# Seven products in more k-groups of two feed-forwards, later flips, output chunks between the pairs

## The chip, the cores and the metric

One core of one Trainium2 chip runs the whole program. The metric is device time in microseconds, the median of a few runs. The engines are TensorE (PE; its weight loads are listed as PEld), VectorE (DVE), ScalarE (ACT), GpSimd (POOL) and SyncE (SP), which issues the DMAs.

## What is computed

Two transformer blocks on 256 tokens of width 2048 in float32, one after the other, on the same `x`. The first block is a sliding-window attention and a SwiGLU feed-forward. The second is a hybrid mixer (gated linear attention and a pooling branch), a cross attention over a memory of 256 rows, a feed-forward with a short convolution, and a last normalisation. The change touches the two feed-forwards, both of width 5632:

```python
def swiglu(h, w_gate, w_up, w_down):
    return (jax.nn.silu(h @ w_gate) * (h @ w_up)) @ w_down

def conv_glu_ffn(h, w_up, conv_w, conv_b, w_down):
    u = h @ w_up
    u = lax.conv_general_dilated(u, conv_w[:, None, :], ...) + conv_b
    gate, val = u[..., :D_FF_2], u[..., D_FF_2:]
    return (jax.nn.silu(gate) * val) @ w_down
```

## The kernel before

**Float32 as three products.** Every large operand is split into a high part, rounded to the fp32r type, and the rest. `mm` (line 263) issues three matmuls for one k-tile of 128 rows and one half of the tokens (128): high x high, high x rest, rest x high (lines 270 to 272), each with 512 columns of weights as the moving operand.

**Units, tasks and ticks.** The weights come in units of 1 MB (512 rows of k by 512 columns). `plan` writes down the order of all units by hand, once; `load_ahead` issues their DMAs on SP into four raw buffers. Half a unit is a task: `split_ahead` casts it (ScalarE, line 225, into `wh`) and subtracts (VectorE, line 226, into `wl`), into five buffers each, three tasks ahead of the one in use. TensorE's order is the order of the code. The order of the other engines is made by a planner from priorities and modelled durations. Small work (transposes, softmax, convolution) runs as jobs: generators that are stepped once per `tick`, one tick per k-tile of the matrix multiplication, or per product. A job that yields 3 is stepped again three ticks later.

**A feed-forward before.** Its 11 chunks of 512 hidden columns each need a gate chunk and an up chunk (4 units each, the four k-groups of the width 2048). `PARTS1` and `PARTS2` group the chunks; after each group of hidden chunks, the four output chunks of the group before are computed (`w_dn1`, `w_dn2`, one unit per hidden chunk of the group) and added to `x` (`add_x`, line 451). The last group's output chunks go with the next norm or the end of the program.

**The pair.** In the first feed-forward, chunks 1 to 10 are computed by `pair`: gate and up chunk together, into four PSUM banks `p2`, `p4`, `p5`, `p3`. With A the activations of one k-group cut into token halves and k halves, and the units of gate and up as the columns, one k-group is a two by two product of blocks. In groups 0 to 2 it is taken with eight block products, in the last group with seven (Strassen's scheme in Winograd's form): sums and differences of blocks of activations (`differences`, once per feed-forward) and of weights (`form`, lines 242 to 246, four operations of VectorE in place in the raw buffers) are multiplied in seven products of two k-tiles each, one task each. Three of the products go to further banks (two `aux`, one `po`), are added with the four accumulators in the order of lines 357 to 373, and give silu's input and the up rows in four tiles. In `swiglu`, line 787 applies silu and line 774 multiplies; `group_job` then turns the rows (four transposes of TensorE in `flip`, line 405, twice) and splits them (lines 387, 388). It first yields 3.

**The second feed-forward before** uses `gemm` with plain groups for all its chunks. ScalarE scales the rows out of PSUM (line 420); `conv_job` waits 3 ticks, turns the rows, and does the taps (lines 1139 to 1142), silu, the product (line 1154) and the split.

**Buffers that the change touches.** PSUM has four banks `acc`, three `aux`, one `po`. The pool `s4` has 21 tiles of 4 KB per partition (groups of activations, sums of activations), `s2` has 12 tiles of 2 KB (rows, results of the pair, results of the convolution).

Of the kernel before, what the change touches and what calls it, by code (L numbers as in the profile page):

```python
# [10 lines left out]
F32 = mybir.dt.float32  # L11
F32R = mybir.dt.float32r
I32 = mybir.dt.int32
AF = mybir.ActivationFunctionType
# [69 lines left out]
class _Net:  # L84
# [71 lines left out]
    def units(w, n, ks=range(4)):  # L156
        return [(w, n, k) for k in ks]

    def plan(self):
# [7 lines left out]
        def pair(a, b):  # L167
            for g in range(len(a)):
                if g == len(a) - 1:
                    self.seven.add(len(p))  # L170
                p.extend((b[g], a[g]))

        def ffn(gate, up, off, down, parts, seven=False):
            prev = None
            for ks in parts:
                for c in ks:
                    if seven and c:
                        pair(U(gate, c), U(up, c + off))
                    else:
                        add([U(gate, c), U(up, c + off)], c == 0)  # L180
                if prev:
                    add([U(down, n, prev) for n in range(4)])
                prev = ks
            add([U(down, n, prev) for n in range(4)])

        add([U("w_qkv", n) for n in (4, 0, 1, 2, 3)])
        add([U("w_o", n) for n in range(4)], True)
        ffn("w_gate", "w_up1", 0, "w_dn1", PARTS1, True)
# [9 lines left out]
        ffn("w_up2", "w_up2", 11, "w_dn2", PARTS2)  # L198
        return p

    def load_ahead(self, n):
# [86 lines left out]
                    done(banks[c])  # L288
                self.tick()

    def differences(self, acts):


        nc = self.nc
        out = []
        for g, z in enumerate(acts):
            h, l = z = self.need(z)
            f = self.s4([128, 4, 256])
            nc.vector.tensor_add(f, h.bitcast(F32), l.bitcast(F32))
            p, q = f[:, :, 0:128], f[:, :, 128:256]  # L300
            yield 2
            if g < len(acts) - 1:
                hl = self.s4([128, 2, 4, 128], F32R)
                nc.vector.tensor_sub(p, p, q)
                nc.scalar.copy(hl[:, 0], p)
                nc.vector.tensor_sub(hl[:, 1], p, hl[:, 0].bitcast(F32))
                out.append((hl[:, 0], hl[:, 1]))
            else:
                s = self.s4([128, 8, 128])
                nc.vector.tensor_add(s[:, 0:2], q[:, 0:2], q[:, 2:4])  # L310
                nc.vector.tensor_sub(s[:, 2:4], s[:, 0:2], p[:, 0:2])
                nc.vector.tensor_sub(s[:, 4:6], p[:, 0:2], q[:, 0:2])
                nc.vector.tensor_sub(s[:, 6:8], p[:, 2:4], s[:, 2:4])
                yield 1
                h, l = (self.s4([128, 8, 128], F32R) for _ in range(2))
                nc.scalar.copy(h, s)
                nc.vector.tensor_sub(l, s, h.bitcast(F32))
                out.append((h, l))
            yield 2
        return out  # L320

    def pair(self, left, right, acts, diffs):

        nc = self.nc
        acts = [self.need(z) for z in acts]
        p2, p4, p5, p3 = (self.bank(tag="acc") for _ in range(4))
        last = len(acts) - 1  # L330
        for g in range(last):
            for units in (right, left):
                for k, w in enumerate(self.weights(units[g])):
                    f = g == 0 and k == 0
                    if units is left:
                        self.mm(p2, acts[g], k, 0, w, f, False)
                        self.mm(p4, acts[g], k, 1, w, f, False)
                    else:
                        self.mm(p5, acts[g], k, 1, w, f, False)
                        self.mm(p3, diffs[g], k, 0, w, f, False)  # L340
                    self.tick()
        assert self.stream[self.used:self.used + 2] == [right[last], left[last]]
        self.used += 2
        A, S = acts[last], diffs[last]

        def product(o, z, k, t, start):
            h, l = self.task()
            for i in range(2):
                self.mm(o, z, k + i, t, (h[:, i], l[:, i]), start and i == 0, i == 1)
            self.tick()  # L350

        add = nc.vector.tensor_add
        u, a, b, c = (self.s2([128, 512]) for _ in range(4))
        product(p3, S, 6, 0, False)
        o = self.bank()
        product(o, A, 0, 0, True)
        nc.scalar.copy(u, o)
        product(p2, A, 2, 0, False)
        add(a, p2, u)
        yield a  # L360
        o = self.bank()
        product(o, S, 2, 0, True)
        add(u, o, u)
        product(p5, S, 0, 0, False)
        add(b, p5, u)
        add(b, p3, b)
        yield b
        o = self.bank(tag="po")
        product(o, S, 4, 0, True)
        add(u, o, u)  # L370
        product(p4, A, 2, 1, False)
        add(c, p4, u)
        add(u, p5, u)
        yield c
        yield u
# [384 lines left out]
    def swiglu(self):  # L760
        nc, a = self.nc, self.a
        r, xacts = self.r, self.xacts

        def up(c, late):
# [12 lines left out]

            if c == 0:
                self.gemm([(self.units(w, c), f) for w, f in (("w_gate", on_gate), ("w_up1", on_up))],
                          xacts, late=late)  # L780
                diffs.append(self.spawn(self.differences(xacts)))
                return hid[0]
            diffs[0] = self.need(diffs[0])
            U = []
            for i, z in enumerate(self.pair(self.units("w_gate", c), self.units("w_up1", c), xacts, diffs[0])):
# [7 lines left out]
        self.ffn(up, "w_dn1", PARTS1, lambda *z: self.residual(*z, "g_mix_2"))  # L793

    def ffn(self, up, w, parts, last):

        prev = None
        for p in parts:
            hid = [up(c, late=c == 0) for c in p]
            if prev:  # L800
                self.residual(w, *prev, None)
            prev = (p, hid)
        last(w, *prev)


    def mixer(self):
# [320 lines left out]
    def conv_ffn(self):  # L1127
        nc, a = self.nc, self.a
        xacts, r, vec = self.xacts, self.r, self.vec
# [14 lines left out]
            return y  # L1144

        def conv_job(c, rows):
            yield 3
            hl = self.group()
            for k in (0, 2):
                yg = conv(rows[0], c, k)  # L1150
# [5 lines left out]
                yield 1  # L1156
            return hl

        def up(c, late):
            rows, hid = [], []  # L1160

            def on_gate(p):
# [2 lines left out]
            def on_val(p):  # L1165
# [1 line left out]
                hid.append(self.spawn(conv_job(c, rows)))  # L1167

            self.gemm([(self.units("w_up2", c + 11 * j), f)
                       for j, f in enumerate((on_gate, on_val))], xacts, late=late)  # L1170
            return hid[0]

        self.ffn(up, "w_dn2", PARTS2, self.final)

    def final(self, w, ks, acts):

# [115 lines left out]
```

## Time and profile before

| | us |
|---|---|
| median of 3 runs | 2728.22 (2726.79 to 2728.71) |
| profiled execution, its own time | 2726.57 |
| its span | 2724.7 |

The span goes from the first to the last instruction. A line of a timeline has the start, the duration, the engine, the line of the kernel, the operation with its output and inputs, the count, and in brackets the idle time of the engine before it and what ended that. Recorded matmuls overlap, since each starts before the end of the one before it: the distance of two starts is the time that one takes.

The stages of the span, in us from its start: the first feed-forward from about 281 to 985, the mixer and the cross attention to 1990, the second feed-forward to 2722.

### The profile page before, as it was taken

The page shows a single profiled execution, that of the slowest core. Times are in us where ns is not written, and L with a number is a line of the kernel's source. Part 1 is how long each engine was busy: PE and PEld are TensorE (multiplying, and loading weights), DVE is VectorE, ACT ScalarE, POOL GpSimd, SP SyncE. Part 2 cuts the span into 40 slices and gives each one's busy share as a digit, 9 for nine tenths or more (in the row PEclk, how much of TensorE's full clock was granted, in tenths as well). Part 3 has the DMA queues.
Part 4 walks back from the last instruction along what each step waited for, and adds up shares of the span by engine and source line. Part 5 has one row for each costly group of instructions (what it writes and reads, how often), then busy time and mean ns, then how long its engine had stood idle before and what let it go on. Part 6 is the DMA issues. An engine that isn't in the chain of part 4 may idle for free.

```text
span 2724.7 us, 31400 instructions
## 1 busy us (share of the span) xinstructions
PE 2684.9 (99%) x12472; PEld 2218.8 (81%) x12472; DVE 1669.1 (61%) x1981; ACT 1354.5 (50%) x1775; POOL 27.1 (1%) x27
## 2 busy tenths in 40 slices
PE   8999999999999999999999999999999999999998
PEld 7778888787878888888888888888888888888887
DVE  7775677767676764745545555554565656556565
ACT  6555554444444454544444455444555554554543
POOL 0000000000000000000000000000000000000000
PEclk9999999999999999999999999999999999999999
DMA  7334545555555555445555556444555555555553
GB/s 302 109 124 155 187 166 194 204 178 199 185 193 179 200 185 184 161 164 181 190 188 197 184 206 227 171 158 168 185 186 185 186 185 187 189 191 190 185 201 124
DMA packets 74083, 499.60 MB, mean 183 GB/s; under 512 B 8496, under 2 KB 9392, under 8 KB 14928
## 3 DMA queue, kind: packets, MB, share of 16 engines
q1 hardware_dynamic: 73936, 497.59, 51.1%
q8 instruction: 98, 1.61, 0.2%
q14 instruction: 49, 0.40, 0.0%
HBM read 495.46 MB, written 2.10 MB: 183 GB/s over the span
## 4 chain that ended last, share of the span: by engine, by line
PE 91%; DVE 4%; issue 2%; DMA 1%; ACT 1%; POOL 1%; SPq 0%; DVEq 0%; POOLq 0%; ACTq 0%
PE acc L270 28%; PE acc L272 28%; PE acc L271 28%; PE aux L405 2%; PE po L718 1%; DMA raw<-in_w_qkv 1%; DVE s L774 1%; POOL sm L429 1%; DMA x<-in_x 0%; PE aux L272 0%; PE aux L271 0%; PE aux L270 0%; DVE wl L226 0%; PE aux L949 0%; PE aux L679 0%
## 5 line engine op out<-in xcount | busy, mean ns | idle before, releaser
L226 DVE TENSOR_TENSOR wl<-raw,wh 128x1024 fp32r<-128x1024 f32 (+1 forms) x952 | 1160.7, 1221 | 961.1 <-ACT wh L225 959.4
L225 ACT CAST wh<-raw 128x1024 fp32r<-128x1024 f32 (+1 forms) x952 | 997.8, 1050 | 1175.8 <-PE acc L272 1154.7
L270 PE MATMUL acc<-wh,s 128*128 128x512 f32 x3600 | 1425.5, 396 | 6.5 <-ACT wh L225 5.6
L272 PE MATMUL acc<-wh,s 128*128 128x512 f32 x3600 | 1404.6, 390 | 0.6 <-DVE s L388 0.6
L271 PE MATMUL acc<-wl,s 128*128 128x512 f32 x3600 | 1403.3, 390 | 0.3 <-DVE wl L226 0.3
L270 PEld LDWEIGHTS acc<-wh,s 128*128 128x128 f32 x3600 | 676.9, 188 | 147.2 <-ACT wh L225 5.6
L272 PEld LDWEIGHTS acc<-wh,s 128*128 128x128 f32 x3600 | 676.3, 188 | 144.8 <-DVE s L388 1.1
L271 PEld LDWEIGHTS acc<-wl,s 128*128 128x128 f32 x3600 | 677.4, 188 | 134.2 <-DVE wl L226 1.4
L405 PE MATMUL aux<-con,s 128*128 128x128 f32 x408 | 63.1, 273 | 15.6 <-DVE s L774 15.6
L405 PEld LDWEIGHTS aux<-con,s 128*128 128x128 f32 x408 | 50.2, 140 | 31.5 <-DVE s L774 19.1
L420 ACT ACTIVATE s<-acc,sm 128x512 f32<-128x512 f32 x72 | 48.9, 689 | 33.3 <-PE acc L272 33.3
L451 DVE TENSOR_TENSOR x<-acc,x 128x512 f32<-128x512 f32 x96 | 61.7, 681 | 0.0
L387 ACT CAST s<-aux 128x512 fp32r<-128x512 f32 x66 | 38.3, 584 | 40.3 <-PE aux L405 30.1
L1139 ACT ACTIVATE s<-aux,vec 128x256 f32<-128x256 f32 x88 | 48.1, 560 | 13.5 <-PE aux L405 8.3
L429 POOL TENSOR_TENSOR sm<-sm,mhalf 128x2 f32<-128x2 f32 (+3 forms) x22 | 26.0, 1182 | 2691.2 <-DVE sm L437 2354.3
L388 DVE TENSOR_TENSOR s<-aux,s 128x512 fp32r<-128x512 f32 x66 | 44.7, 685 | 10.5 <-ACT s L387 9.4
L392 ACT ACTIVATE s<-aux,vec 128x256 fp32r<-128x256 f32 x80 | 37.7, 473 | 22.3 <-PE aux L405 13.9
L1140 DVE SCALAR_TENSOR_TENSOR s<-aux,vec,s 128x255 f32<-128x255 f32 x88 | 41.1, 477 | 2.6 <-ACT s L1139 0.2
L393 DVE SCALAR_TENSOR_TENSOR s<-aux,vec,s 128x256 fp32r<-128x256 f32 x80 | 38.2, 481 | 6.7 <-ACT s L392 5.4
L1142 DVE SCALAR_TENSOR_TENSOR s<-aux,vec,s 128x254 f32<-128x254 f32 x88 | 40.1, 477 | 1.2
L692 ACT ACTIVATE s<-s,sm 128x128 f32<-128x128 f32 (+1 forms) x64 | 28.3, 444 | 13.7 <-DVE sm L687 13.7
L426 ACT ACTIVATE s<-x 128x512 f32<-128x512 f32 (+1 forms) x44 | 29.1, 663 | 9.8 <-DVE x L1187 9.3
(194 smaller groups left out, 965.4 us busy)
## 6 DMA issues: line engine op xcount, KB each, us to landing
raw<-in_w_up SPq DMA_DIRECT2D x132, 1024.0 KB, 4.7
raw<-in_w_dn SPq DMA_DIRECT2D x88, 1024.0 KB, 4.8
raw<-in_w_in SPq DMA_DIRECT2D x64, 1024.0 KB, 4.7
raw<-in_w_gate SPq DMA_DIRECT2D x44, 1024.0 KB, 4.7
raw<-in_w_ckv SPq DMA_DIRECT2D x32, 1024.0 KB, 4.7
raw<-in_w_qkv SPq DMA_DIRECT2D x19, 1024.0 KB, 6.0
raw<-in_w_o SPq DMA_DIRECT2D x16, 1024.0 KB, 4.8
raw<-in_w_br SPq DMA_DIRECT2D x16, 1024.0 KB, 4.8
```

The costliest lines, as they stand in the source:

```text
L225: nc.scalar.copy(h[:, m], raw[:, m])
L226: nc.vector.tensor_sub(l[:, m], raw[:, m], h[:, m].bitcast(F32))
L270: nc.tensor.matmul(o, ah[:, k, s], h, start=first, stop=False)
L271: nc.tensor.matmul(o, ah[:, k, s], l, start=False, stop=False)
L272: nc.tensor.matmul(o, al[:, k, s], h, start=False, stop=last)
L388: nc.vector.tensor_sub(l[:, k0:k0 + n], src, h[:, k0:k0 + n].bitcast(F32))
L405: self.nc.tensor.transpose(b[:, j, t * 128:t * 128 + 128], srcs[t][:, (k + j) * 128:(k + j) * 128 + 128], self.ident)
L420: self.nc.scalar.activation(dst[t], pss[t], AF.Identity, bias=0.0, scale=sc[:, t:t + 1])
L429: self.nc.gpsimd.tensor_tensor(out, var, self.mhalf[:, :n], op=ALU.pow)
L451: nc.vector.tensor_add(xs[t], pss[t], xs[t])
L1139: nc.scalar.activation(y[:, j], b[:, j], AF.Identity, bias=bb, scale=w2)
L1140: nc.vector.scalar_tensor_tensor(y[:, j, 1:256], b[:, j, 0:255], w1, y[:, j, 1:256], op0=ALU.mult, op1=ALU.add)
```

## The change

- `SEVEN1 = (1, 3)`: in the first feed-forward's pairs, k-groups 1 and 3 are taken with seven products, where it was group 3 alone. The three further banks then accumulate over both groups (from group 1 to the end of group 3), and are read in the last.
- `SEVEN2 = (3,)`: chunks 1 to 10 of the second feed-forward are computed by `pair` too, with group 3 in seven products; ScalarE scales the four results in place. `differences` runs there once as well. Its results for plain groups lie in two tiles of `s2` each, where it was half an `s4` tile for each part.
- Both feed-forwards use the same `PARTS`, and `ffn_steps` puts the output chunks of a group between the pairs of the next group, two after each pair, where all four came after the last pair. The second feed-forward's groups have two chunks, where they had three.
- The jobs that turn the rows first yield 8, where it was 3 (except for chunk 0).

```diff
-PARTS1 = ((0,), (1, 2), (3, 4), (5, 6), (7, 8), (9, 10))
-PARTS2 = ((0, 1, 2), (3, 4, 5), (6, 7, 8), (9, 10))
+PARTS = ((0,), (1, 2), (3, 4), (5, 6), (7, 8), (9, 10))
+SEVEN1, SEVEN2 = (1, 3), (3,)
...
+    def ffn_steps():
+        prev = None
+        for ks in PARTS:
+            for i, c in enumerate(ks):
+                yield c, None, None
+                if prev:
+                    for n in range(4 * i // len(ks), 4 * (i + 1) // len(ks)):
+                        yield None, n, prev
+            prev = ks
...
-            if g < len(acts) - 1:
-                hl = self.s4([128, 2, 4, 128], F32R)
+            if g not in seven:
+                h, l = (self.s2([128, 4, 128], F32R) for _ in range(2))
...
+        o1 = None
+        for g in range(len(acts)):
+            A, S = acts[g], diffs[g]
+            if g not in seven:
+                for units in (right, left):
+                    outs = ((p2, A, 0), (p4, A, 1)) if units is left else ((p5, A, 1), (p3, S, 0))
+                    for k, w in enumerate(self.weights(units[g])):
+                        for o, z, t in outs:
+                            self.mm(o, z, k, t, w, id(o) not in used, False)
+                            used.add(id(o))
+                        self.tick()
+                continue
+            assert self.stream[self.used:self.used + 2] == [right[g], left[g]]
+            self.used += 2
+            if o1 is None:
+                o1, o6, o7 = self.bank(), self.bank(), self.bank(tag="po")
+            end = g == seven[-1]
+            product(p3, S, 6, 0, end)
+            product(o1, A, 0, 0, end)
+            if end:
+                u, a, b, c = (self.s2([128, 512]) for _ in range(4))
+                nc.scalar.copy(u, o1)
+            product(p2, A, 2, 0, end)
...
-                hid.append(self.spawn(self.group_job(silu)))
+                hid.append(self.spawn(self.group_job(silu, wait=3 if c == 0 else 8)))
...
+        for c, n, ks in self.ffn_steps():
+            if n is None:
+                hid[c] = up(c)
+                continue
+            self.gemm([(self.units(w, n, ks), lambda pss: self.add_x(n, pss, None))], [hid[k] for k in ks])
...
         def conv_job(c, rows):
-            yield 3
+            yield 3 if c == 0 else 8
...
+        def up7(c):
+            if c == 0:
+                hid = up(c)
+                diffs.append(self.spawn(self.differences(xacts, SEVEN2)))
+                return hid
+            diffs[0] = self.need(diffs[0])
+            rows = [[], []]
+            for i, z in enumerate(self.pair(self.units("w_up2", c), self.units("w_up2", c + 11),
+                                            xacts, diffs[0], SEVEN2)):
+                nc.scalar.activation(z, z, AF.Identity, bias=0.0, scale=r[:, i // 2:i // 2 + 1])
+                rows[i % 2].append(z)
+            return self.spawn(conv_job(c, rows))
```

## Rows read from the trace of the kernel before

**Rows 1.** The page: engines' busy time and instructions; the chain's shares by engine.
```profile
PE 2684.9 (99%) x12472; PEld 2218.8 (81%) x12472; DVE 1669.1 (61%) x1981; ACT 1354.5 (50%) x1775; POOL 27.1 (1%) x27
...
PE 91%; DVE 4%; issue 2%; DMA 1%; ACT 1%; POOL 1%; SPq 0%; DVEq 0%; POOLq 0%; ACTq 0%
```

**Rows 2.** Stretches: busy time and instructions per engine, granted clock, DMA share, GB/s.
```profile
281.00:985.00 704.00, 688.44 (x3065) 565.04 (x3064) 493.07 (x497) 332.71 (x350) 0.49 (x1) 1.00 0.52 189
...
1990.00:2722.00 732.00, 725.95 (x3287) 600.79 (x3286) 436.90 (x524) 368.68 (x450) 1.10 (x2) 1.00 0.52 183
2257.00:2361.00 104.00, 104.00 (x460) 86.04 (x460) 56.99 (x59) 45.13 (x48) 0.00 (x0) 1.00 0.53 188
...
283.00:325.00 42.00, 42.00 (x186) 34.68 (x186) 31.73 (x37) 22.33 (x25) 0.00 (x0) 1.00 0.52 185
```

**Rows 3.** Waits over the whole span: us in total, times, longest.
```profile
PE aux L405 <- DVE s L774: 15.6, 10, 1.6
...
PEld acc L270 <- DVE s L366: 3.5, 10, 0.4
```

**Rows 4.** Timeline of TensorE where the first pair ends and the second begins.
```profile
365.39 0.39 PE L270 MATMUL acc<-wh,s 128*128 128x512 f32 x1
...
365.84 0.39 PE L272 MATMUL acc<-wh,s 128*128 128x512 f32 x1
366.16 0.50 PE L270 MATMUL acc<-wh,s 128*128 128x512 f32 x1
...
369.72 0.27 PE L405 MATMUL aux<-con,s 128*128 128x128 f32 x1
371.55 0.55 PE L405 MATMUL aux<-con,s 128*128 128x128 f32 x3 [1.56 <-DVE s L774]
```

**Rows 5.** Timeline of TensorE at a flip of the second feed-forward.
```profile
2255.71 0.60 PE L405 MATMUL aux<-con,s 128*128 128x128 f32 x4
2256.07 0.47 PE L270 MATMUL acc<-wh,s 128*128 128x512 f32 x1
```

**Rows 6.** Timeline of TensorE: the same place after the third and the fifth pair.
```profile
478.15 0.50 PE L270 MATMUL acc<-wh,s 128*128 128x512 f32 x1
...
611.92 0.50 PE L270 MATMUL acc<-wh,s 128*128 128x512 f32 x1
```

**Rows 7.** Timeline of VectorE from the first seven-product group on.
```profile
346.27 1.23 DVE L226 TENSOR_TENSOR wl<-raw,wh 128x1024 fp32r<-128x1024 f32 x1 [1.50 <-ACT wh L225]
347.53 1.22 DVE L242 TENSOR_TENSOR raw<-raw 128x1024 f32<-128x1024 f32 x1
348.79 1.23 DVE L243 TENSOR_TENSOR raw<-raw,raw 128x1024 f32<-128x1024 f32 x1
...
360.82 1.21 DVE L226 TENSOR_TENSOR wl<-raw,wh 128x1024 fp32r<-128x1024 f32 x1
...
370.75 0.74 DVE L774 SCALAR_TENSOR_TENSOR s<-s,sm,s 128x512 f32<-128x512 f32 x1
...
377.84 1.22 DVE L226 TENSOR_TENSOR wl<-raw,wh 128x1024 fp32r<-128x1024 f32 x1 [1.38 <-ACT wh L225]
```

**Rows 8.** Timeline of ScalarE as TensorE enters that group.
```profile
356.12 1.05 ACT L225 CAST wh<-raw 128x1024 fp32r<-128x1024 f32 x1 [1.68 <-PE acc L272]
357.48 1.05 ACT L225 CAST wh<-raw 128x1024 fp32r<-128x1024 f32 x1 [0.31 <-PE acc L272]
```

**Rows 9.** Timeline of SP's queue: the loads issued during that group.
```profile
359.81 0.33 SPq L205 DMA_DIRECT2D raw<-in_w_up  x1
362.06 0.33 SPq L205 DMA_DIRECT2D raw<-in_w_gate  x1
```

**Rows 10.** DMA issues by kind: KB each, median us to landing.
```profile
raw<-in_w_up SPq DMA_DIRECT2D x132, 1024.0 KB, 4.7
```

**Rows 11.** Groups by form: busy us, mean ns of one, idle before and its releasers.
```profile
L226 DVE TENSOR_TENSOR wl<-raw,wh 128x1024 fp32r<-128x1024 f32 x948 | 1158.0, 1223 | 958.1 <-ACT wh L225 956.5
...
L243 DVE TENSOR_TENSOR raw<-raw,raw 128x1024 f32<-128x1024 f32 x10 | 12.3, 1225 | 0.3
...
L363 DVE TENSOR_TENSOR s<-aux,s 128x512 f32<-128x512 f32 x10 | 6.8, 683 | 0.0
```

More of the change, by code (lines that the diff above doesn't have):

```diff
@@ L165, in add, with pair, ffn @@
             p.extend(chunks[c][g] for c, g in self.order(chunks, late))
-        def pair(a, b):
+        def pair(a, b, seven):
             for g in range(len(a)):
-                if g == len(a) - 1:
+                if g in seven:
                     self.seven.add(len(p))
                 p.extend((b[g], a[g]))
[L173 to L184, printed above, removed]
+        def ffn(gate, up, off, down, seven):
+            for c, n, ks in self.ffn_steps():
+                if n is not None:
+                    add([U(down, n, ks)])
+                elif c:
+                    pair(U(gate, c), U(up, c + off), seven)
+                else:
+                    add([U(gate, c), U(up, c + off)], True)
+            add([U(down, n, PARTS[-1]) for n in range(4)])
         add([U("w_qkv", n) for n in (4, 0, 1, 2, 3)])
         add([U("w_o", n) for n in range(4)], True)
-        ffn("w_gate", "w_up1", 0, "w_dn1", PARTS1, True)
+        ffn("w_gate", "w_up1", 0, "w_dn1", SEVEN1)
         add([U("w_in", n) for n in (0, 1)], True)
@@ L289, in gemm, with differences @@
                 self.tick()
-    def differences(self, acts):
+    def differences(self, acts, seven):
         nc = self.nc
@@ L301, in differences @@
             yield 2
[L302 to L303 removed]
+            if g not in seven:
+                h, l = (self.s2([128, 4, 128], F32R) for _ in range(2))
                 nc.vector.tensor_sub(p, p, q)
[L305 to L307 removed]
+                nc.scalar.copy(h, p)
+                nc.vector.tensor_sub(l, p, h.bitcast(F32))
             else:
@@ L317, in differences, with pair, product @@
                 nc.vector.tensor_sub(l, s, h.bitcast(F32))
-                out.append((h, l))
+            out.append((h, l))
             yield 2
         return out
-    def pair(self, left, right, acts, diffs):
+    def pair(self, left, right, acts, diffs, seven):
         nc = self.nc
+        add = nc.vector.tensor_add
         acts = [self.need(z) for z in acts]
         p2, p4, p5, p3 = (self.bank(tag="acc") for _ in range(4))
[L330 to L346, printed above, removed]
+        used = set()
+        def product(o, z, k, t, stop):
@@ L347, in product @@
             h, l = self.task()
             for i in range(2):
-                self.mm(o, z, k + i, t, (h[:, i], l[:, i]), start and i == 0, i == 1)
+                self.mm(o, z, k + i, t, (h[:, i], l[:, i]), id(o) not in used, stop and i == 1)
+                used.add(id(o))
             self.tick()
[L352 to L371, printed above, removed]
+        o1 = None
[7 more added lines that the diff above has]
+                            self.mm(o, z, k, t, w, id(o) not in used, False)
+                            used.add(id(o))
+                        self.tick()
[11 more added lines that the diff above has]
+            product(p2, A, 2, 0, end)
+            if end:
+                add(a, p2, u)
+                yield a
+            product(o6, S, 2, 0, end)
+            if end:
+                add(u, o6, u)
+            product(p5, S, 0, 0, end)
+            if end:
+                add(b, p5, u)
+                add(b, p3, b)
+                yield b
+            product(o7, S, 4, 0, end)
+            if end:
+                add(u, o7, u)
+            product(p4, A, 2, 1, end)
@@ L762, in swiglu, with up @@
         r, xacts = self.r, self.xacts
-        def up(c, late):
+        def up(c):
             silu, hid = [], []
@@ L784, in up @@
             U = []
-            for i, z in enumerate(self.pair(self.units("w_gate", c), self.units("w_up1", c), xacts, diffs[0])):
+            for i, z in enumerate(self.pair(self.units("w_gate", c), self.units("w_up1", c),
+                                            xacts, diffs[0], SEVEN1)):
                 if i % 2 == 0:
@@ L792, in swiglu, with ffn @@
         diffs = []
[L793 to L803, printed above, removed]
+        self.ffn(up, "w_dn1", lambda *z: self.residual(*z, "g_mix_2"))
+    def ffn(self, up, w, last):
+        hid = {}
+        for c, n, ks in self.ffn_steps():
+            if n is None:
+                hid[c] = up(c)
+                continue
+            self.gemm([(self.units(w, n, ks), lambda pss: self.add_x(n, pss, None))], [hid[k] for k in ks])
+            if n == 3:
+                for k in ks:
+                    del hid[k]
+        last(w, PARTS[-1], [hid.pop(k) for k in PARTS[-1]])
     def mixer(self):
@@ L1157, in conv_job, with up @@
             return hl
-        def up(c, late):
+        diffs = []
+        def up(c):
             rows, hid = [], []
@@ L1169, in up, with last @@
             self.gemm([(self.units("w_up2", c + 11 * j), f)
-                       for j, f in enumerate((on_gate, on_val))], xacts, late=late)
+                       for j, f in enumerate((on_gate, on_val))], xacts, late=True)
             return hid[0]
-        self.ffn(up, "w_dn2", PARTS2, self.final)
+        def up7(c):
[10 more added lines that the diff above has]
+            return self.spawn(conv_job(c, rows))
+        def last(*z):
+            diffs.clear()
+            xacts.clear()
+            self.final(*z)
+        self.ffn(up7, "w_dn2", last)
     def final(self, w, ks, acts):
```

7 lines of the change are left out of this document (4 added, 3 removed).

## Prediction

> **What bounds the kernel now.** I read the page's busy times first, then a table by stretches, the list of waits, and last the timelines around one pair of chunks. The page gives TensorE 99% busy and 91% of the chain that ended last; VectorE has 61%, ScalarE 50% [rows 1]. Since recorded matmuls overlap, 99% alone proves little. The stretches do: where there is nothing but 512-column matmuls, 460 are seen in 104.00 us, one of them cut at the edge, so one starts every 104 / 459 = 0.2266 us [rows 2]. In the second feed-forward TensorE is busy 725.95 of 732 us, while VectorE works 436.90; in the first it is 688.44 of 704 with VectorE at 493.07 [rows 2]. The clock is at its upper level (1.00) in all of them. So a removed matmul is worth its 0.2266 us as long as VectorE and ScalarE, which cast the weights, stay ahead.
>
> The 15.6 us that TensorE idles in the first feed-forward are one wait, ten times: the transposes of the hidden rows (line 405) wait for VectorE's product at line 774 [rows 3]. In the first pair: the pair's last matmul ends where the next group starts, 365.39; three ticks later the first transpose starts at 369.72, the next only at 371.55, because line 774 runs at 370.75 [rows 4, 7]. A second, smaller wait sits at each pair's end: the bank that line 366 reads. The start at 365.84 is followed by one at 366.16 instead of 366.07, and the following step is slow by another 0.1: 0.2 us in all [rows 3, 4].
>
> **The change part by part.**
>
> *Matmuls.* A plain k-group of a pair is 2 units x 4 k-tiles x 2 halves of the tokens x 3 = 48 matmuls; as seven products it is 7 x 2 x 3 = 42. The first feed-forward gets a second such group in 10 pairs, the second gets one in 10 pairs: 120 matmuls go, 60 in each. 120 x 0.2266 = 27.2 us, all on the path. The matmul count should fall from 12472 to 12352. The Trainium skill ("TensorE: Matmul & The Clock Gate", Part 1, "Wait — 56ns, not 53.3ns?") gives 215.7 ns start to start for 512 columns, by which these would be worth 25.9 us; the trace's 0.2266 does not agree and decides.
>
> *Flips eight ticks on.* A tick after a pair is 6 matmuls (1.36 us). Eight instead of three put the first transpose 8 x 1.36 = 10.9 us after the pair's end instead of 4.1. Line 774 starts its second half 5.4 us after that end (370.75 - 365.39) and lasts 0.74 [rows 7], so the rows are there 4.8 us early. An unhindered flip takes 2256.07 - 2255.71 = 0.36 us for four transposes [rows 5], 0.09 each; the stalled step takes 1.83. Gain 1.74 x 10 = 17.4 us. Between 0 and 17.4, I take all of it, since the row names line 774 and nothing else. The hidden chunk is needed a whole output chunk or more later: nothing new is late.
>
> *Second seven-product group: VectorE.* It adds four combinations of weights (lines 242 to 246, 1.225 us each) and three more casts (1.22 on VectorE, 1.05 on ScalarE). One pair with its two output chunks then asks of VectorE 30 casts x 1.223 + 8 x 1.225 + the pair's end 7 x 0.68 + 1.5 (line 774) + 1.4 (line 388) + 4 x 0.68 (adds to x) = 56.9 us, while TensorE has 276 x 0.2266 + 0.9 + 0.2 = 63.6 [rows 2, 11]. It fits on average; the question is the place. In the trace the seven-product group begins on TensorE at 365.39 - 42 x 0.2266 = 355.87. VectorE starts its first cast at 346.27, 9.6 us earlier, and ends the seventh at 360.82 + 1.21 = 362.03, where TensorE needs it at 355.87 + 6 x 1.36 = 364.03: 2.0 us in hand [rows 7]. What paces the casts are the five cast buffers: ScalarE's cast at 357.48 waits for a product to free one [rows 8]. In the new order 7-product groups stand at places 1 and 3 with one plain group (10.9 us, 4 casts) between. With the first group's start as 0: VectorE is through with its seventh cast at +6.2 (no pair's end there), with the plain group's casts, again paced by buffers, by about +10.7; the third group's first cast can start when product six frees its buffer at +9.5, so it runs at +10.6 to +11.8 and the combinations at +11.8 to +17. TensorE reaches that group at +20.4, i.e. 9.8 us after that first cast, as in the trace. So the second group meets the lead that the only one has now. Cost 0; with the lead wholly lost it would be 13.5 us of VectorE work (7 casts at about 1.2, 4 combinations at 1.25) against 9.5 of TensorE: 4.0 per pair, 40 us in all. I take 0.
>
> *Its loads.* The two raw units of the second group can load only when the first group's two are free: the trace issues such loads at 359.81 and 362.06, +3.9 and +6.2, and they land 4.7 us later, at +8.6 and +10.9 [rows 9, 10]. The combination that needs the second unit follows another at about +13, so 2 us are free, and about 4 more before a product is late. Cost 0, for a landing up to 6 us slower too; nothing here can gain, as TensorE does not wait for loads today. SP's queue issues them in the same order of units; behind a waiting load stand only later loads.
>
> *The same in the second feed-forward.* Its pairs are three plain groups and one of seven, then two output chunks: what the first feed-forward does now, without a stall inside. New there: a pair ends with seven adds (ten times 4.8 us of VectorE; the copy beside them is ScalarE's), 16 more adds to x (10.9 us), the sums and differences of the activations once. That last piece stands in the stretch 283 to 325 today: VectorE 31.73 of 42, TensorE 42.00 [rows 2], so chunk 0 hides it. VectorE goes from 436.9 to about 593 of some 718 us, 83%; covered. On the path comes the bank wait at the pair's end, nearest row 0.2 us: +2.0 (0 to 2 by where the banks fall). The same wait in the first feed-forward stays.
>
> *Second feed-forward's flips.* They come in the second output chunk, four in four ticks. Now they pass without a gap. The pool of twelve 2 KB tiles then holds six of differences, four of rows and only two for the convolution; the fourth flip needs the bank of the first. Between 0 (as now) and 1.74 each (as in the first feed-forward), I take 0: the first flip's bank is free once the convolution's first output is written, and for that there is a tile.
>
> *Sum.* -27.2 - 17.4 + 2.0 = -42.6. The profiled execution took 2726.6, so 2684.0; it lies 1.6 under the median 2728.2, so a median of 2685.
>
> **Rivals.**
>
> *The gap moves.* If the flips lack a buffer rather than the data, they stall wherever they stand: -42.6 + 17.4 = -25.2, 2702. For it: it is the same length ten times. Against: the releaser is line 774 each time [rows 3], and the second feed-forward's flips use the same banks without a gap. The Trainium skill ("Perfetto Trace Analysis", Identifying the Most-Contended Engine) says that a gap repeating on the engine that should be saturated can mean too few buffers; by that rule this case holds, but the trace names data.
>
> *The second feed-forward's flips wait* for VectorE, which has two adds to x ahead of them, or for tiles: +1.74 x 10, 2702. For it: only two tiles are left. Against: lead as above.
>
> *VectorE loses part of its lead* at the second seven-product group: 1 to 2 us per pair, +10 to +20, 2695 to 2705.
>
> *Slower: VectorE paces both seven-product groups of each first-feed-forward pair.* Place: the cast of products three to seven. Price with no lead at all: 4.0 us in the first, and 4.0 + 5 x 0.60 of pair's-end adds in the second, 11 us a pair, 110 us: 2795. It turns the sign when a pair loses more than 42.6 / 10 = 4.3 us. For it: 13.5 us of VectorE work in 9.5 of TensorE, twice within 30 us. Against: VectorE is idle again at 377.84 for lack of work, 12 us after the pair's end [rows 7], and the groups are separated by plain ones.
>
> **How the numbers follow.** Forecast 0.75; the gap moves 0.05; flips of the second feed-forward wait 0.08; part of the lead lost 0.07; slower 0.05. About 5.5 us (0.2%) is what a measurement of this kernel can tell from no change; all cases but the last are far beyond it. Faster 0.93, same 0.02, slower 0.05. Range: below, 2677 (no bank wait at any pair's end, -4, and a few small steps after stalls that go too); above, 2706, which takes in the four faster cases; only the slower one is out, and stretches between.
>
> **What would show it.** Matmuls 12352. No wait of line 405 on line 774, or its successor. A pair of the first feed-forward with its two output chunks repeating every 276 x 0.2266 + 1.1 = 63.6 us, against (611.92 - 478.15) / 2 = 66.9 now [rows 6]. First feed-forward 32 us shorter at its end, second 11 to 12. TensorE waiting for line 226 or 225 inside pairs, first or second group, would show the VectorE rivals; a gap before a flip in the second feed-forward the tile one. A total above 2706, or TensorE idle over 10 us in either feed-forward, makes the prediction wrong.

## The result, and the profile after

| | before | after | difference |
|---|---|---|---|
| median of the runs shown beside each other, us | 2727.51 | 2686.98 | -40.5 |
| profiled execution: own time, span, us | 2726.57, 2724.7 | 2686.66, 2684.5 | -39.9, -40.2 |
| first feed-forward, us | 703.35 | 671.82 | -31.5 (forecast -31.0) |
| between the two, us | 994.78 | 994.78 | 0 |
| second feed-forward, us | 746.01 | 737.79 | -8.2 (forecast -11.6) |
| matmuls | 12472 | 12352 | -120 |

The ratio is 0.9852 [0.9835, 0.9869]. The forecast was 2685, so it missed by 2 us. The first feed-forward is measured here from chunk 0's first transpose to the first transpose of its last step's output chunk; the second one from the first transpose of the cross attention's last output chunk to the end of the span. The same landmarks serve for every kernel below. What stands ahead of the first one, which no edit touches, took 280.1 to 283.0 us in the traces, and the median of the kernel before was 2725.9 to 2727.5 from one batch of runs to the next; so differences of a few us are read from the feed-forwards' own times. In two of the experiments one execution took 8.4 or 11.9 ms, far outside the other runs of its kernel, and is left out.

The page after, busy times and the chain's shares, against [rows 1]:

```profile
PE 2657.9 (99%) x12352; PEld 2195.2 (82%) x12352; DVE 1890.7 (70%) x2225; ACT 1424.2 (53%) x1849; POOL 27.1 (1%) x27
...
PE 97%; DVE 2%; ACT 1%; POOL 0%; DMA 0%; issue 0%; SPq 0%; POOLq 0%; DVEq 0%; ACTq 0%
```

TensorE's busy time fell by 27.0 us, close to the 27.2 reckoned for 120 matmuls; the other 13 us are idle time that went. VectorE took on 221.6 us of work, and its share of the chain fell all the same, from 4% to 2%, while that of TensorE rose from 91% to 97%.

Stretches after (columns as in [rows 2]): the first feed-forward, then the second.

```profile
280.50:952.30 671.80, 671.80 (x3003) 553.74 (x3001) 576.40 (x570) 363.92 (x380) 0.55 (x1) 1.00 0.53 197
1952.00:2684.00 732.00, 721.35 (x3254) 593.23 (x3252) 577.23 (x697) 408.40 (x497) 1.10 (x2) 1.00 0.51 185
```

In the first, TensorE's records now cover all 671.80 us (688.44 of 704 before): the ten gaps are gone. In the second, 10.65 of 732 us are uncovered, against 6.05 before. Of these, 8.2 lie behind the last matmul (6.05 before, where the stretch ends 2.2 us nearer to it); the other 2.4 are two waits that are new. VectorE works 86% and 79%.

Waits after, the lists of TensorE and of its weight loads, against [rows 3] (us in total, times, longest):

```profile
PE aux L421 <- DVE s L1162: 1.8, 1, 1.8
...
PE acc L280 <- ACT s L315: 0.6, 1, 0.6
...
PEld acc L280 <- DVE s L382: 7.1, 20, 0.4
```

The ten waits of the transposes on line 774 (now 790) are gone. The small wait at each pair's end, 0.35 us on the weight load, came to the second feed-forward as forecast: 20 times instead of ten. The first two rows are new, both at the start of the second feed-forward's first pair; they are most of the miss there, and the experiment that asks for the differences earlier takes them apart.

TensorE after: the same place in two successive pairs of the first feed-forward, against [rows 6].

```profile
533.80 0.50 PE L280 MATMUL acc<-wh,s 128*128 128x512 f32 x1
...
597.53 0.50 PE L280 MATMUL acc<-wh,s 128*128 128x512 f32 x1
```

A pair with its two output chunks takes 63.7 us (forecast 63.6; 66.9 before).

VectorE after, as the first pair enters its second seven-product group, against [rows 7] (that group begins on TensorE at 354.06).

```profile
345.73 1.22 DVE L252 TENSOR_TENSOR raw<-raw 128x1024 f32<-128x1024 f32 x1
346.99 1.22 DVE L253 TENSOR_TENSOR raw<-raw,raw 128x1024 f32<-128x1024 f32 x1
...
359.02 1.22 DVE L236 TENSOR_TENSOR wl<-raw,wh 128x1024 fp32r<-128x1024 f32 x1
...
368.94 0.75 DVE L790 SCALAR_TENSOR_TENSOR s<-s,sm,s 128x512 f32<-128x512 f32 x1
```

The first combination starts 8.3 us before the group; before the change it was also 8.3 (347.53 against 355.87). The lead is the old one, though a second such group stands 20 us ahead. The rows' product at line 790 still ends 6.1 us after the pair's last matmul (369.69 - 363.58; 371.49 - 365.39 before); only the transpose no longer stands there waiting.

### The profile page after: what moved, and what is told of

It reads as the page before. It is cut to its first block, busy times and chain, and to the rows that moved or that the text cites. A ratio compares the mean times of both kernels' runs of the same rounds, so it can differ in the third digit from the quotient of the medians.

```text
span 2684.5 us, 31592 instructions
## 1 busy us (share of the span) xinstructions
PE 2657.9 (99%) x12352; PEld 2195.2 (82%) x12352; DVE 1890.7 (70%) x2225; ACT 1424.2 (53%) x1849; POOL 27.1 (1%) x27
## 4 chain that ended last, share of the span: by engine, by line
PE 97%; DVE 2%; ACT 1%; POOL 0%; DMA 0%; issue 0%; SPq 0%; POOLq 0%; DVEq 0%; ACTq 0%
PE acc L280 29%; PE acc L282 29%; PE acc L281 29%; PE aux L421 2%; PE aux L282 1%; PE aux L281 1%; PE aux L280 1%; PE po L734 1%; PE po L282 1%; PE po L281 1%; PE po L280 1%; PE aux L969 0%; POOL sm L445 0%; DVE wl L236 0%; DMA raw<-in_w_qkv 0%; PE aux L695 0%
## 5 line engine op out<-in xcount | busy, mean ns | idle before, releaser
L236 DVE TENSOR_TENSOR wl<-raw,wh 128x1024 fp32r<-128x1024 f32 (+1 forms) x1012 | 1230.7, 1220 | 689.0 <-ACT wh L235 677.1
L235 ACT CAST wh<-raw 128x1024 fp32r<-128x1024 f32 (+1 forms) x1012 | 1060.2, 1051 | 1084.0 <-PE acc L282 1020.6
L280 PE MATMUL acc<-wh,s 128*128 128x512 f32 x3440 | 1364.1, 397 | 7.4 <-ACT wh L235 5.5
L282 PE MATMUL acc<-wh,s 128*128 128x512 f32 x3440 | 1342.6, 390 | 0.6 <-DVE s L404 0.6
L281 PE MATMUL acc<-wl,s 128*128 128x512 f32 x3440 | 1341.0, 390 | 0.4 <-DVE wl L236 0.4
L280 PEld LDWEIGHTS acc<-wh,s 128*128 128x128 f32 x3440 | 646.9, 188 | 145.5 <-DVE s L382 7.1
L282 PEld LDWEIGHTS acc<-wh,s 128*128 128x128 f32 x3440 | 646.2, 188 | 138.1 <-DVE s L404 1.1
L281 PEld LDWEIGHTS acc<-wl,s 128*128 128x128 f32 x3440 | 647.3, 188 | 128.2 <-DVE wl L236 1.7
L467 DVE TENSOR_TENSOR x<-acc,x 128x512 f32<-128x512 f32 x112 | 72.8, 682 | 0.0
L280 PE MATMUL aux<-wh,s 128*128 128x512 f32 x120 | 46.7, 389 | 0.0
L281 PE MATMUL aux<-wl,s 128*128 128x512 f32 x120 | 46.7, 389 | 0.0
L282 PE MATMUL aux<-wh,s 128*128 128x512 f32 x120 | 46.7, 389 | 0.0
```

Source lines behind the costliest of these rows:

```text
L235: nc.scalar.copy(h[:, m], raw[:, m])
L236: nc.vector.tensor_sub(l[:, m], raw[:, m], h[:, m].bitcast(F32))
L280: nc.tensor.matmul(o, ah[:, k, s], h, start=first, stop=False)
L281: nc.tensor.matmul(o, ah[:, k, s], l, start=False, stop=False)
L282: nc.tensor.matmul(o, al[:, k, s], h, start=False, stop=last)
L467: nc.vector.tensor_add(xs[t], pss[t], xs[t])
```

## The experiments

The ratio is to the kernel before, timed beside each; differences are between the profiled spans, to the kernel before for the first one and to the kernel after for the others.

**The transposes later, alone** (on the kernel before)

```diff
-hid.append(self.spawn(self.group_job(silu)))
+hid.append(self.spawn(self.group_job(silu, wait=3 if c == 0 else 8)))
```

> The kernel before with one edit: the job that turns the hidden rows of the first feed-forward's pairs yields 8 ticks instead of 3. Theory (TensorE waited for the data of line 774, which comes 5.4 to 6.1 us after a pair's end): all ten waits go, 17.4 us less than before, about 2710. Rival (the flip lacks a buffer, the gap moves along): 2727, with a gap of about 1.7 us at the later flip.

Measured: 2708.87, 0.9937 [0.9923, 0.9950]; the span fell by 17.6 us, the median by 17.1. No wait on line 774 is left, nothing else moved, and the waits at line 366 stayed (3.5 us, ten times). That the gap went with the same number of buffers speaks for late data; alone it would also fit a buffer that comes free late. The trace of before rules that out: the four transposes of a flip go into one bank (`flip`), and the first of them was in it at 369.72, 1.83 us before the stalled three [rows 4]. The Trainium skill's rule ("Perfetto Trace Analysis", Optimization Strategy) that a repeating gap on the engine that should be saturated can mean too few buffers does not apply to this one.

**The first feed-forward's second group taken back** (on the kernel after)

```diff
-SEVEN1, SEVEN2 = (1, 3), (3,)
+SEVEN1, SEVEN2 = (3,), (3,)
```

> The changed kernel with group 3 alone in seven products in the first feed-forward (60 matmuls come back, all else stays). Theory (VectorE hides the second group wholly): 60 x 0.2266 = 13.6 us slower than the changed kernel, about 2700.5. Rival (the second group costs VectorE's lead something): less than 10 us slower.

Measured: 2700.85, 0.9906 [0.9893, 0.9920]. The span is 14.6 longer, the median 13.9, the first feed-forward 13.8 (685.59 against 671.82). In its stage the group is worth its 60 matmuls (13.6), to 0.2 us: VectorE's added work for it cost nothing there.

**The second feed-forward plain again** (on the kernel after)

```diff
-SEVEN1, SEVEN2 = (1, 3), (3,)
+SEVEN1, SEVEN2 = (1, 3), ()
...
-        self.ffn(up7, "w_dn2", last)
+        self.ffn(up, "w_dn2", last)
```

(and its chunks, but for the first, with both units of a k-group in their plain order again.)

> The changed kernel with the second feed-forward's chunks all plain again (no seven products there, its differences not computed; order of chunks and late flips stay). Theory (each matmul is worth its 0.2266 us, ten bank waits of 0.2 us and about 3.3 us at the start of that feed-forward came with the pairs): 13.6 - 2.0 - 3.3 = 8.3 us slower than the changed kernel, about 2695. Rival (VectorE's added work in the second feed-forward also costs time that no gap shows, or the start would be late anyway): 2 us slower or less, or 13 and more.

Measured: 2699.14, 0.9900 [0.9886, 0.9913]; the second feed-forward is 11.2 us longer, more than the 8.3 expected. A part is this variant's own: the first transpose of each chunk starts later than it does elsewhere,

```profile
PEld aux L421 <- issue: 5.1, 10, 0.5
```

0.27 us on TensorE, ten times: 2.7 us. Without it 8.5 remain, near the 8.2 between the kernels before and after. What makes that first transpose late is not settled.

**Output chunks after the pairs again** (on the kernel after)

```diff
-            for i, c in enumerate(ks):
+            for c in ks:
                 yield c, None, None
-                if prev:
-                    for n in range(4 * i // len(ks), 4 * (i + 1) // len(ks)):
-                        yield None, n, prev
+            if prev:
+                for n in range(4):
+                    yield None, n, prev
```

> The changed kernel with the four output chunks after the last pair of a group, as before, instead of two after each pair; the same work. Theory (VectorE is behind by some 6 us when a pair ends, one plain group of 10.9 us is all that the next pair's first seven-product group then has ahead of it, and its products four to seven come 0.5 to 2 us late): gaps of TensorE waiting for lines 236 or 235 in the second pair of five groups of the first feed-forward, none in the second one, 5 to 12 us slower than the changed kernel, 2692 to 2699. Rival (the place of the output chunks does nothing): 2687.

Measured: 2689.26, 0.9863 [0.9850, 0.9877], the span 1.6 us longer, the first feed-forward 0.6 (672.40) and the second 0.3: a miss in size. Two pairs then follow each other directly, and TensorE's weight loads do wait for casts in the second one,

```profile
PEld acc L281 <- DVE wl L236: 3.0, 9, 0.7
```

but five of these nine, 1.1 us in all and 0.2 at most, are in the first feed-forward and none in the second; the other four stand elsewhere, as four do in the kernel after (1.7 us). A loss of 5 to 12 had been expected. The order of the chunks is nearly free here.

**The transposes soon again** (on the kernel after)

```diff
-hid.append(self.spawn(self.group_job(silu, wait=3 if c == 0 else 8)))
+hid.append(self.spawn(self.group_job(silu, wait=3)))
...
-            yield 3 if c == 0 else 8
+            yield 3
```

> The changed kernel with the flips back at 3 ticks after a pair, in both feed-forwards. Theory (the wait is for the data of the pair's end, line 790 in this kernel, wherever seven products end a pair): the first feed-forward's ten gaps of 1.7 us come back, 17.4 us; in the second the rows are ready only after VectorE's seven adds and ScalarE's scaling, about 4 to 6 us after the pair's end against 4.1 us of ticks, so up to 2 us each there, 0 to 20: 17 to 37 us slower than the changed kernel, 2704 to 2724. Rival (with output chunks behind the pairs VectorE is free sooner, the flips could stand at 3): 2687.

Measured: 2724.62, 0.9993 [0.9984, 1.0002]: nearly the whole gain of the change is gone. The first feed-forward is 18.0 us longer, the second 19.2.

```profile
PE aux L421 <- DVE s L790: 15.8, 10, 1.6
PE aux L421 <- ACT wh L235: 9.7, 8, 1.2
PE acc L280 <- ACT wh L235: 5.7, 1, 5.7
PE aux L421 <- DVE s L1162: 3.7, 3, 1.8
...
PE aux L421 <- ACT s L1204: 3.5, 10, 0.4
```

The first row is the old wait. The second, fourth and fifth are the transposes of the second feed-forward, which passed without a gap before the change [rows 5]: after a seven-product pair they would have waited too (one of the fourth row's three, 1.8 us, is chunk 0's flip, which waits in the kernel after as well). So the eight ticks protect two stages, though the second one's wait never stood in the trace of before. (The third row, once, is in the kernel after too, with 5.5 us.)

**The differences before chunk 0** (on the kernel after, in both feed-forwards)

```diff
-                hid = up(c)
                 diffs.append(self.spawn(self.differences(xacts, SEVEN2)))
-                return hid
+                return up(c)
```

> The changed kernel with one edit in each feed-forward: the job of the differences is spawned before chunk 0's matrix multiplication instead of behind it, so that its 2 KB tiles come before those of chunk 0's rows in the program's order. Theory (the casts of the plain groups' differences start late, at 1989 us, because their tiles are handed out behind the rows' tiles, while VectorE and ScalarE idle in chunk 0; the first pair's first product and chunk 0's fourth flip of the second feed-forward wait for that, 0.8 + 0.2 + 2.0 us): 3.0 us less than the changed kernel, about 2684, and line 315 runs inside chunk 0. Rival (the pool of twelve tiles is simply full then, or the convolution's own work delays the flip): the flip's wait stays, 1 us less or nothing.

Measured: 2683.86, 0.9844 [0.9830, 0.9857], -3.1 by the medians (by the spans 0.7, as what stands ahead of the first feed-forward took 2.1 us longer in this trace); the second feed-forward is 737.79 - 734.66 = 3.1 shorter. The kernel after first, TensorE where its second feed-forward's first pair begins:

```profile
1988.89 0.39 PE L282 MATMUL acc<-wh,s 128*128 128x512 f32 x1
1989.88 0.50 PE L280 MATMUL acc<-wh,s 128*128 128x512 f32 x1 [0.60 <-ACT s L315]
...
1997.60 0.40 PE L282 MATMUL acc<-wh,s 128*128 128x512 f32 x1
1999.84 0.63 PE L421 MATMUL aux<-con,s 128*128 128x128 f32 x4 [1.84 <-DVE s L1162]
```

The steps take 0.99 and 2.24 us instead of 0.23: 2.8 of the 3.4 that the forecast missed. ScalarE of that kernel at the same place:

```profile
1987.96 1.37 ACT L436 ACTIVATE s<-acc,sm 128x512 f32<-128x512 f32 x2 [0.99 <-PE acc L282]
1989.22 0.61 ACT L315 CAST s<-s 128x512 fp32r<-128x512 f32 x1
1989.73 1.05 ACT L235 CAST wh<-raw 128x1024 fp32r<-128x1024 f32 x1
1990.68 1.14 ACT L315 CAST s<-s 128x512 fp32r<-128x512 f32 x2
```

and its VectorE, which had long been through with what those casts read:

```profile
1958.81 0.69 DVE L314 TENSOR_TENSOR s<-s 128x512 f32<-128x512 f32 x1
...
1971.01 1.22 DVE L236 TENSOR_TENSOR wl<-raw,wh 128x1024 fp32r<-128x1024 f32 x1 [1.78 <-ACT wh L235]
...
1989.86 0.69 DVE L316 TENSOR_TENSOR s<-s,s 128x512 fp32r<-128x512 f32 x1 [1.63 <-ACT s L315]
```

The differences are formed by 1959.5; VectorE has gaps from 1969 on; yet the casts run at 1989, right behind chunk 0's rows (line 436). Their results are 2 KB tiles of the pool from which chunk 0's four rows also come, and in program order the rows were asked for first. That it is these tiles, and not the job or the engine that was late, shows in the cast of group 3's sums: it belongs to the same job, comes behind the others in it, has tiles of the 4 KB pool, and ran 24 us before them.

```profile
1965.16 1.05 ACT L325 CAST s<-s 128x1024 fp32r<-128x1024 f32 x1
```

With the differences asked for first, in this experiment:

```profile
1954.65 0.62 ACT L315 CAST s<-s 128x512 fp32r<-128x512 f32 x1
1955.77 1.06 ACT L235 CAST wh<-raw 128x1024 fp32r<-128x1024 f32 x1 [0.49 <-PE acc L282]
1958.47 1.06 ACT L235 CAST wh<-raw 128x1024 fp32r<-128x1024 f32 x1 [1.65 <-PE acc L282]
1959.69 0.62 ACT L315 CAST s<-s 128x512 fp32r<-128x512 f32 x1 [0.15 <-DVE s L314]
```

they run more than 30 us earlier, and both waits go: the fourth flip passes at 1999.09 in its step of 0.23.

**p3 read before p5 at a pair's end** (on the kernel after)

```diff
                 add(u, o6, u)
+                add(b, p3, u)
             product(p5, S, 0, 0, end)
             if end:
-                add(b, p5, u)
-                add(b, p3, b)
+                add(b, p5, b)
```

> The changed kernel with the order of two additions at a pair's end changed: bank p3, complete with the first of the seven products, is read as soon as the sum of the two further products is there, and p5 is added to that afterwards. Theory (the 0.2 us at each of 20 pairs' ends is the wait for line 382's reading of p3, which stands behind the product p5): all 20 go, 4.0 us less than the changed kernel, about 2683. Rival (the next chunk's second bank would be the late one anyway, the wait passes to line 386 or 388): nothing.

Measured: 2687.45, 0.9854 [0.9839, 0.9869]: no change, where -4 was expected. The 20 bank waits went, and the first feed-forward is 2.3 shorter (669.51). But the second is 1.6 longer:

```profile
PE aux L421 <- DVE s L1162: 5.5, 3, 1.8
```

Behind the first and the second pair, too, TensorE now finds line 1162 unfinished at the fourth flip. What changed there is VectorE's order. In the kernel after, at the first pair's flips, it runs three pairs of taps (lines 1160 and 1162) and then a cast, and the fourth flip starts at 2052.28 without a wait:

```profile
2051.61 0.48 DVE L1162 SCALAR_TENSOR_TENSOR s<-aux,vec,s 128x254 f32<-128x254 f32 x1
2052.01 1.22 DVE L236 TENSOR_TENSOR wl<-raw,wh 128x1024 fp32r<-128x1024 f32 x1
```

Here that cast, which itself waits for ScalarE's, stands ahead of the third pair of taps, and the fourth flip waits until 2051.92:

```profile
2049.38 1.23 DVE L236 TENSOR_TENSOR wl<-raw,wh 128x1024 fp32r<-128x1024 f32 x1 [0.61 <-ACT wh L235]
...
2051.30 0.86 DVE L1162 SCALAR_TENSOR_TENSOR s<-aux,vec,s 128x254 f32<-128x254 f32 x2
```

The second pair has the same; in the third the old order stands again, without a wait. So ten waits of 0.2 us were traded for two of 1.8. Why the planner's order changed is not shown.

**The same, with the second feed-forward's flips two ticks apart** (on the one just told)

```diff
                 nc.scalar.activation(yg, yg, AF.Silu)
-                yield 1
+                yield 2
...
                 self.split(hl, k, yg)
-                yield 1
+                yield 2
```

> The kernel of e6_p3_read_first with one more edit: the convolution job's four flips stand two ticks apart, not one. Theory (e6 saved its 20 x 0.2 us and gave them back in two fourth flips of the second feed-forward that wait for VectorE's line 1162, after pairs 1 and 2; with two ticks between them the taps of the first flip are through in time, and chunk 0's fourth flip, 2.0 us, is free too): 4.0 + 2.0 = 6 us less than the changed kernel, about 2681. Rival (the waits pass to another place again): 2685 to 2687.

Measured: 2681.53, 0.9836 [0.9822, 0.9849], -5.5 to the kernel after, close to the 6 expected. No trace of this kernel is read, so that the waits at the fourth flip went is not shown; the time agrees with it.

**Two seven-product groups in the second feed-forward too** (on the kernel after)

```diff
-SEVEN1, SEVEN2 = (1, 3), (3,)
+SEVEN1, SEVEN2 = (1, 3), (1, 3)
```

> The changed kernel with k-groups 1 and 3 in seven products in the second feed-forward too: 60 matmuls less, 13.6 us. By durations VectorE then has 9.8 + 26.8 + 4.8 + 10.4 + 12.5 = 64.3 us to do per pair and two output chunks, TensorE 64.5. Theory (VectorE's starts lie closer than its durations, 1.14 us for a cast of 1.22, so it still fits; up to 0.4 us lost a pair): 9.6 to 13.6 us less than the changed kernel, 2673 to 2677. Rival (VectorE goes by its durations and paces the pairs, with the convolution delaying casts): 5 us less or none, with TensorE waiting for line 236 or 235 by 1 us and more a pair.

Measured: 2678.25, 0.9821 [0.9808, 0.9835], -8.7: between the two expectations. 60 matmuls are worth 13.6; 4.9 were lost. Busy times in the second feed-forward, and in its second pair:

```profile
1946.00:2680.00 734.00, 715.91 (x3228) 587.24 (x3226) 659.33 (x778) 442.05 (x537) 1.80 (x3) 1.00 0.50 186
...
2050.00:2110.00 60.00, 56.39 (x258) 45.67 (x257) 58.50 (x74) 38.30 (x48) 0.00 (x0) 1.00 0.47 175
```

VectorE is at 90% over the stage, but at 58.50 of 60 us in that pair, where TensorE is short by 3.6. The larger losses stand in the first three pairs only, again two more flips behind line 1162 and two late casts, by the starts of the steps 1.83 and 0.45 us each.

**Three seven-product groups in the first feed-forward** (on the kernel after)

```diff
-SEVEN1, SEVEN2 = (1, 3), (3,)
+SEVEN1, SEVEN2 = (1, 2, 3), (3,)
```

> The changed kernel with k-groups 1, 2 and 3 in seven products in the first feed-forward: 60 matmuls less, 13.6 us, but no plain group between. Theory (the plain group between is what gives VectorE its lead and the raw buffers their time: 39.3 us of VectorE work meet 28.6 of TensorE, and the next group's two loads land 8.6 and 10.9 us after a group's start where TensorE needs the third product's weights 12.2 us after it): 4 to 6 us lost a pair, 2713 to 2733, TensorE waiting for line 236 or 235 in groups 2 and 3. Rival (there is lead to spare): 2673.

Measured: 2738.18, 1.0042 [1.0029, 1.0054], slower than the kernel before and 51 us above the kernel after; more than the 46 at the end of what was expected.

```profile
ACT wh L235 <- DVE raw L254: 69.4, 23, 4.5
...
PE aux L281 <- DVE wl L236: 19.7, 20, 1.2
PE aux L280 <- ACT wh L235: 18.9, 10, 2.1
```

This is what the slower rival describes, with one group more: casts of adjacent seven-product groups come too late, three times in each pair. They are late by VectorE's combinations (the first row), not by the loads, for which ScalarE's casts wait 5.4 us in the whole first feed-forward. Two stretches inside the first pair show what it costs beyond the waits:

```profile
358.00:362.50 4.50, 1.42 (x6) 0.64 (x4) 4.47 (x6) 3.02 (x5) 0.00 (x0) 1.00 0.00 0
362.50:367.00 4.50, 4.50 (x13) 3.55 (x14) 4.50 (x5) 3.81 (x6) 0.00 (x0) 0.62 0.29 62
```

VectorE is full in both. TensorE works 1.42 of 4.50 us, and in the next stretch its granted clock is 0.62.

**The three gains together** (differences first, p3 read first with the flips two ticks apart, and two groups in the second feed-forward)

> The changed kernel with all of it: differences early, p3 read first, seven products in groups 1 and 3 of the second feed-forward, convolution flips two ticks apart. Theory: -3.1 (e5) - 4.0 (p3) - 13.6 (60 matmuls) + some 1 to 2 us of casts late in groups 1 and 3 of the second feed-forward's first pairs = 2667 to 2669. Rival (VectorE at about 97% of the second feed-forward's pairs loses its lead with the order of work changed): 2673 to 2680.

Measured: 2673.81, 0.9808 [0.9795, 0.9822]: 13.2 us below the kernel after and the best version, though 5 to 7 us above the theory and inside the rival's range (2673 to 2680). The first feed-forward is 2.3 us shorter than in the kernel after, the second 11.9 (725.85).

```profile
PE aux L281 <- DVE wl L236: 1.7, 1, 1.7
...
PE po L281 <- DVE wl L236: 1.2, 1, 1.2
...
PE aux L280 <- ACT wh L235: 1.1, 2, 0.6
```

These are casts late in the first three pairs of the second feed-forward. Up to the third pair the output chunks between the pairs are one unit long, later two, which leaves VectorE less room; that this is the reason was not tested.

## Why the prediction was right, and where it was off

*Matmuls, -27.2.* Confirmed one stage at a time: one group taken back costs 13.9 by the median and 13.8 in its stage, against 13.6. In the second feed-forward the experiment gives 11.2, of which 2.7 are that variant's own; the 8.5 left, with the 2.0 of bank waits and the 2.8 of waits at its start that the pairs brought, make 13.3.

*Flips eight ticks on, -17.4.* Confirmed alone, at 17.1. The rival that the gap only moves is out. But the step was undersold: with the seven-product pairs in both feed-forwards the later flips carry 37.6 us, since the second one's flips would have begun to wait. The forecast priced the eight ticks in the first feed-forward alone. In the second it took the flips at nothing, as they were before, and did not say that it is the eight ticks that keep them so.

*Second group: VectorE's lead, 0, and its loads, 0.* Confirmed: the lead is 8.3 us as before, and the first feed-forward came out 31.5 shorter against the 31.0 of the forecast's terms (its last paragraph says 32). The lead does not hold by much: three groups in place of two lost 6.5 us a pair ((51.2 + 13.6) / 10), more than the 5.4 a pair ((40.5 + 13.6) / 10) that there was to lose, and the kernel was slower than before. (The forecast's 4.3 is the same turn for two groups.) Two such groups fit because a plain one stands between.

*Bank wait at the second feed-forward's pair ends, +2.0.* The ten waits appeared, as long as the old ones. Taking all 20 away shortened the first feed-forward by 2.3 for ten.

*The differences in the second feed-forward, 0.* This is the term that was mis-sized. "So chunk 0 hides it" looked at busy time: 31.73 of 42 us [rows 2]. The work was there and had room, but its tiles were not: they were handed out behind chunk 0's rows, the casts ran more than 30 us late, and the first pair's first product and chunk 0's fourth flip waited. It measured 3.1 us, nearly all of the 3.4 by which the second feed-forward missed. The forecast had counted the 2 KB tiles ("six of differences, four of rows and only two for the convolution") but only for the flips; the count was the right one, and the order in which they are asked for was what mattered.

*Second feed-forward's flips, 0.* Right for all ten pairs, with the eight ticks. The one flip that waits is chunk 0's, just told.

*The signs.* One of them, "TensorE idle over 10 us in either feed-forward", is met to the letter by the 10.65 us above, though the time lies well inside the range. It was a poor sign: 8.2 of the 10.65 stand behind the last matmul, as in the kernel before, and the new idle time is 2.4.

## What to carry to other kernels

A wait that repeats on the busiest engine and names one line of late data can be cured by asking later, if something else can run in between; and the same delay can guard a stage where the wait does not show yet. When work is costed at nothing because another chunk hides it, look also at which of the two asks the pool first: free engines do not help a tile that is handed out late. A feeding engine at 90% of a stage can stand at 97% of one pair in it, and there a part of the next saving is lost.

## What the runs showed of the hardware

With three adjacent seven-product groups, TensorE's clock fell. Its matmuls there, after waits of 1.84 and 1.24 us with one matmul between them:

```profile
360.67 0.50 PE L280 MATMUL aux<-wh,s 128*128 128x512 f32 x1 [1.84 <-ACT wh L235]
362.41 0.50 PE L281 MATMUL aux<-wl,s 128*128 128x512 f32 x1 [1.24 <-DVE wl L236]
...
363.86 0.63 PE L280 MATMUL acc<-wh,s 128*128 128x512 f32 x1
364.29 0.63 PE L281 MATMUL acc<-wl,s 128*128 128x512 f32 x1
364.71 0.63 PE L282 MATMUL acc<-wh,s 128*128 128x512 f32 x1
```

From 363.44 to 366.85 eight steps take 0.43 us each instead of 0.2266, the lower of the two levels (1.2 GHz), 1.6 us more in all for this one place; over the run the mean granted clock is 0.993, against 0.999 in the kernel after. In the other kernels single waits of 1.8 us, as the one behind line 1162, left the granted clock of their stage at 1.00, and in the version with the three gains together so did waits of 0.62 and 1.68 us with one matmul between (1.00 from 2060 to 2070 us); what tells the two cases apart is not shown. Of the 64.8 us that the three groups lost (51.2 + 13.6), the steps of the first feed-forward beyond 0.2266 us give some 48 us to the 30-odd steps that waited and some 14 to 71 steps at the lower level.
